# A two-layer diffusion backbone on one core: the first layer's feed-forward rebuilt as seven half-block products, with the gated blocks kept in DRAM

## The chip, the cores and the metric

The kernel runs on one core of one Trainium2 chip. The metric is the device time of one execution in microseconds; before the change the median of three runs is 3291.3 us (3287.67 to 3292.95).

## The reference, cut to what matters

Two layers act on 256 context tokens and 1024 latent tokens of width 1024, all in float32. Each layer has an attention, Fourier and recurrence part, and then a gated feed-forward (1024 to 2816 and back). The second layer updates the latent tokens only.

```python
def swiglu(h, wg, wu, wd):
    return (jax.nn.silu(h @ wg) * (h @ wu)) @ wd
for l in range(DEPTH):
    ctx_out = l < DEPTH - 1
    ...
    x = x + g_f * swiglu(rmsnorm(x) * (1 + sc_f) + sh_f, w_gate[l], w_up[l], w_down[l])
    if ctx_out:
        ctx = ctx + mc[5] * swiglu(rmsnorm(ctx) * (1 + mc[4]) + mc[3], w_gate[l], w_up[l], w_down[l])
return rmsnorm(x, final_norm)
```

## The kernel before, in words

Features lie on the 128 partitions and tokens on the free axis, so that the width is 8 tiles (KD) and the inner width 22 (NFF). Tokens come in three chunks (`CHUNKS`): chunk 0 is the context with 256 columns, chunks 1 and 2 are the latent tokens with 512 each. Every operand is split in two fp32r parts, hi and lo, by `split` (L124 to L126: a copy on ScalarE, then a subtraction on VectorE), and `mm3` (L128 to L134) makes three matmuls of each term: hi·hi, hi·lo and lo·hi. A weight block comes in by `slab` (L421): one DMA from the SyncE queue into a `raw` buffer, then the split into the `wh` and `wl` buffers. There are two `raw` buffers (RAWB) and four each of `wh` and `wl` (WB). A `raw` buffer is free again when the subtraction of its split has read it.

The kernel is written as a list of instructions in program order. A planner (the tile framework) puts them into one fixed order on each engine's queue, with the program order as priority and with its own estimates of durations; it inserts the waits, and it may put a DMA far ahead of its use when its buffer is free. The SyncE queue issues all DMAs, in its fixed order.

**Layer 0, feed-forward (`ffn`, L1057).** `out_proj` (L990) makes the residual stream `xT` in SBUF and the normalised operands `hh`, `hl`. Then 11 groups follow, each of 256 of the 2816 inner features. For each of its two 128-feature blocks and for each chunk a group makes `pg` and `pu` (8 terms of three matmuls each), the Silu, the gate product and its split. It then loads two rows of w_down and adds their two terms to each of the 8 output tiles of each chunk (`down`, accumulators `fd`); VectorE adds every such sum to `xT` (`add_residual`, L1049 to L1054). The last group is done in two parts, and the next layer's norm and first projections are put between them (`after`). Between the products, `next(bg)` advances `ada_sums` (L249): it streams 96 blocks of w_ada (256 KB each) through two `wa` buffers and sums them on VectorE (L279, L281), for the second layer's modulation vectors.

**Layer 1, feed-forward (`operands` L1143, `fast_product` L1230, `ffn_last` L1313).** Gate and up are products of a 1024 x 256 weight block with 1024 x 1024 latent activations. Both are cut into halves, and seven products of sums of half blocks stand for eight: B11, B21 and B22 are the activation halves themselves, and T1 to T4 are sums of them, made once in `operands`; sums of weight halves (`mix`) are made for each group. Each product is 4 terms of three 512-column matmuls. The gated results go to DRAM (`da`), and the residual stream does too (`df`). After all 11 groups, the down product is made in two passes, one per latent chunk: the 22 gated tiles come back (`ar`) and are split, and each of the 8 output tiles is accumulated over all 22 terms in one accumulator. The w_down blocks are loaded as slabs of 4 x 128 x 128 (256 KB; the last of each output tile is 128 KB), again in each pass.

```python
1323        for t in range(2):
...
1334            for ds in ((0, 1, 2, 3), (4, 5), (6, 7)) if t == 0 else ((0, 1), (2, 3), (4, 5), (6, 7)):
...
1336                for f0 in range(0, NFF, 4):
```

Of the kernel before, what the change touches and what calls it, by code (L numbers as in the profile page):

```python
# [92 lines left out]
LASTTAGS = ("mx", "sc", "mx", "mm")  # L93
# [7 lines left out]
class Kern:  # L101
# [304 lines left out]

    def norm_chunk(self, tag, l, vsc, vsh, ci, ss):
        self.modulate_chunk(l, vsc, vsh, ci, self.rstd(ss, CHUNKS[ci][1], D, f"{tag}r{ci}", "pa", PAB))
# [581 lines left out]
    def out_proj(self, l):  # L990
# [28 lines left out]
        def block(d, ci):  # L1019
            c0, n = CHUNKS[ci]  # L1020
            hi, lo = slabs[d]
            acc = self.ps("mm", "oacc")
            self.mm3(acc[:, :n], [(hi[k], lo[k], mh[k][:, c0:c0 + n], ml[k][:, c0:c0 + n]) for k in ORDER])
            self.add_residual(l, 2, d, ci, acc)
            self.squares(ss[ci], d, ci)
            if l + 1 == DEPTH:
                nc.sync.dma_start(out=self.df[d][:, c0 - CTX:c0 - CTX + n], in_=self.xT[d][:, c0:c0 + n])


        self.hh, self.hl = mh, ml  # L1030
        if l + 1 == DEPTH:
            for d in range(4):
                slab(d)
                for ci in chunks:
                    block(d, ci)
            self.operands(l, slab, block, ss)
            return
# [6 lines left out]
        for ci in chunks:  # L1044
# [10 lines left out]


    def ffn(self, l, bg, after):  # L1057
        nc = self.nc
        I = self.I
        chunks = (0, 1, 2)  # L1060

        groups = [(g, chunks, "") for g in range(NFF // 2 - 1)]
        groups += [(NFF // 2 - 1, chunks[:2], "last"), (NFF // 2 - 1, chunks[2:], "last")]

        def gate_up(g, i):
            f0 = (2 * g + i) * P
            return [self.slab(I[w][l, :, f0:f0 + P].rearrange("(k p) c -> p k c", p=P), f"{w}{l}_{f0}") for w in ("w_gate", "w_up")]

        first, norms = None, []
        for g, cis, last in groups:  # L1070
            A = {}
            for i in range(2):
                (gh, gl), (uh, ul) = first or gate_up(g, i)
                first = None
                if i and norms:
                    norms.pop()()
                for ci in cis:
                    c0, n = CHUNKS[ci]
                    cs = slice(c0, c0 + n)
                    pg, pu = self.ps("mm", "pg"), self.ps("sc", "pu")  # L1080
                    self.mm3(pg[:, :n], [(gh[k], gl[k], self.hh[k][:, cs], self.hl[k][:, cs]) for k in range(KD)])
                    next(bg, None)
                    self.mm3(pu[:, :n], [(uh[k], ul[k], self.hh[k][:, cs], self.hl[k][:, cs]) for k in range(KD)])
                    sg = self.t2("sg")
                    with self.tc.issue_after(self.last_exp):
                        self.last_silu = nc.scalar.activation(out=sg[:, :n], in_=pg[:, :n], func=AF.Silu).ins
                    nc.vector.tensor_tensor(out=sg[:, :n], in0=pu[:, :n], in1=sg[:, :n], op=ALU.mult)  # L1087
                    if i:
                        A[i, ci] = [self.t2(f"a{p}", F32R, tag="pa", bufs=PAB)[:, :n] for p in "hl"]
                    else:  # L1090
                        t = self.tp.tile([P, 2, 512], F32R, tag="qa", name="a", bufs=QAB)
                        A[i, ci] = [t[:, p, :n] for p in range(2)]
                    self.split(sg[:, :n], *A[i, ci])
                    next(bg, None)
            dn = []
            for i in range(2):
                f0 = (2 * g + i) * P
                dn.append(self.slab(I["w_down"][l, f0:f0 + P, :].rearrange("p (k c) -> p k c", c=P), f"wd{l}_{f0}"))
            tags = itertools.cycle(LASTTAGS)
            if last:  # L1100
                self.load = load = self.exp_ln_set(self.last_silu)

            def down(*blocks, o=0, n=None):
                accs = []
                for i in range(2):
                    for x, (d, ci) in enumerate(blocks):
                        nn = n or CHUNKS[ci][1]
                        if not i:
                            accs.append(self.ps(next(tags) if last else "mx" if ci else "pv", "fd"))
                        self.mm3(accs[x][:, :nn], [(dn[i][0][d], dn[i][1][d], *[y[:, o:o + nn] for y in A[i, ci]])], i == 0, i == 1)  # L1110
                        if i:
                            self.add_residual(l, 5, d, ci, accs[x], o, nn)

            if not last:
                for d in range(KD):
                    if d in (0, KD - 1):
                        down((d, 0), (d, 1), (d, 2))
                    else:
                        for ci in chunks:
                            down((d, ci))  # L1120
            else:
                ss = {}
                for ci in cis:
                    ss[ci] = self.square_acc(ci)
                    for d in range(KD):
                        down((d, ci))
                        self.squares(ss[ci], d, ci)
                if 2 in cis:
                    with self.tc.issue_after(load):
                        self.early_slabs(l + 1)  # L1130
                        self.early_chunk(l + 1, 1, slice(1))
                        norm = after(2, ss[2])
                        self.early_chunk(l + 1, 1, slice(1, 2))
                        norm()
                        self.early_chunk(l + 1, 2)
                else:
                    first = gate_up(g, 0)
                    with self.tc.issue_after(load):
                        norms = [after(ci, ss[ci]) for ci in cis]
                        norms.pop(0)()  # L1140


    def operands(self, l, slab, block, ss):  # L1143
# [21 lines left out]
        for d in range(4, KD):  # L1165
            slab(d)
            block(d, 1)
        slab(4)
        norm(1)
# [8 lines left out]
        puts = self.puts(0)  # L1178
        first = [self.fast_product(l, w, 0, *tb, put, True) for w, tb, put in zip(("w_gate", "w_up"), (("pa", PAB), ("t2", TB)), puts)]
# [33 lines left out]
    def puts(self, g):  # L1213
# [4 lines left out]
        def gate(i, t, x):  # L1218
            gates[i, t] = x
            with self.tc.issue_after(self.last_exp):  # L1220
                self.last_silu = nc.scalar.activation(out=x, in_=x, func=AF.Silu).ins

        def up(i, t, x):
            a = gates[i, t]
            nc.vector.tensor_tensor(out=a, in0=x, in1=a, op=ALU.mult)
            nc.sync.dma_start(out=self.da[2 * g + i][:, 512 * t:512 * t + 512], in_=a)
# [3 lines left out]
    def fast_product(self, l, w, g, tag, bufs, put, early=False):  # L1230


        nc, B = self.nc, self.B
        tags = itertools.cycle(("mm", "sc", "mx", "pv"))
# [31 lines left out]

        def result():
            return self.t2("m" + w, tag=tag, bufs=bufs)
# [5 lines left out]
        p = product(operand(A[0][0]), "11")  # L1274
        nc.scalar.copy(out=x, in_=p)
        p = product(operand(A[0][1]), "21")
        plus(z, p, x)
        if early:
# [8 lines left out]
        put(0, 0, z)  # L1287
# [11 lines left out]
        put(0, 1, v)  # L1299
# [6 lines left out]
        put(1, 1, y)  # L1306
# [4 lines left out]
        put(1, 0, x)  # L1311

    def ffn_last(self, l):  # L1313
        nc = self.nc
# [6 lines left out]
        load = self.exp_ln_set(self.last_silu)  # L1321
        tags = itertools.cycle(("mx", "pv"))
        for t in range(2):
            ts = slice(512 * t, 512 * t + 512)
            a = []
            for f in range(NFF):
                x = self.t2("ar", tag="pa", bufs=PAB)
                nc.sync.dma_start(out=x, in_=self.da[f][:, ts])
                y = self.five(f"a{t}_{f}", F32R, (P, 2, 512))
                a.append((y[:, 0], y[:, 1]))  # L1330
                self.split(x, *a[f])
            rows, X = [], []
            ss = self.t2("ssf", tag="acc", bufs=ACB)
            for ds in ((0, 1, 2, 3), (4, 5), (6, 7)) if t == 0 else ((0, 1), (2, 3), (4, 5), (6, 7)):
# [201 lines left out]
```

## Time and profile before

| what | value |
|---|---|
| median of three runs | 3291.3 us |
| the profiled execution's own time | 3293.05 us |
| its span in the profile | 3291.3 us |
| TensorE busy | 3193.4 us, 97% of the span |
| VectorE, ScalarE, GpSimd busy | 56%, 38%, 4% |
| mean granted TensorE clock | 0.988 |
| DMA | 303.89 MB, 92 GB/s on average |
| layer 0: output projection, feed-forward | from 780 us and from 911 us to about 1856 us |
| layer 1: output projection, feed-forward | from 2479 us and from 2573 us to the end |

The span is the time from the first instruction to the last. A matmul's recorded duration includes its way through the array, so the rate of a row of matmuls is read from the distance between their starts. A busy share near 100% says that the engine has work in its queue all the time; a granted clock below 1.00 says that matmuls then ran at a lower clock for a part of the stretch (1.00 is 2.4 GHz, 0.50 is 1.2 GHz).

### The profile page before, as it was taken

What the parts mean: (1) busy time and instruction counts of PE and PEld (TensorE: products, weight loads), DVE (VectorE), ACT (ScalarE), POOL (GpSimd) and SP (SyncE); (2) the same over time, 40 slices, a digit from 0 to 9 for tenths busy, and PEclk for the clock granted to TensorE, in tenths of its full rate; (3) what the DMA queues carried; (4) which work ended last, traced back from release to release, by engine and by line L of the source; (5) the groups of instructions that cost most, each with busy time, mean ns of one, the idle gap of its engine ahead of it and who ended that gap; (6) DMA issues with size and microseconds to landing.
All of it is one profiled execution on the core that took longest, in us unless ns stands there. A gap on an engine that the chain in (4) does not pass through costs nothing.

```text
span 3291.3 us, 43774 instructions
## 1 busy us (share of the span) xinstructions
PE 3193.4 (97%) x17074; PEld 2366.3 (72%) x17074; DVE 1844.6 (56%) x3230; ACT 1257.4 (38%) x2280; POOL 122.3 (4%) x96
## 2 busy tenths in 40 slices
PE   7999999998999999999999999999999899999998
PEld 4977544455878888888888787644557588887887
DVE  5298766653475353363334737677633876666343
ACT  5255555454331111111112635455453533334343
POOL 1000000000210000000000300000001100000000
PEclk9999999999999999999999999999999899999999
DMA  8346111024122141141112333210125132225453
GB/s 276 109 151 208 54 38 56 20 93 152 39 84 87 42 128 46 38 130 39 39 39 61 122 114 96 73 54 30 31 90 176 58 90 88 82 84 164 147 172 94
DMA packets 284408, 303.89 MB, mean 92 GB/s; under 512 B 16776, under 2 KB 207144, under 8 KB 284200
## 3 DMA queue, kind: packets, MB, share of 16 engines
q1 hardware_dynamic: 284200, 301.09, 29.1%
q8 instruction: 134, 2.20, 0.3%
q14 instruction: 74, 0.61, 0.1%
HBM read 237.18 MB, written 63.70 MB: 91 GB/s over the span
## 4 chain that ended last, share of the span: by engine, by line
PE 83%; DVE 7%; DMA 5%; ACT 3%; issue 2%; POOL 1%; SPq 0%; DVEq 0%; ACTq 0%; POOLq 0%
PE pv L643 6%; PE fd L132 5%; PE fd L133 5%; PE fd L134 5%; PE fp L133 4%; PE fp L132 4%; PE fp L134 4%; PE mx L600 3%; DMA wa<-in_w_ada_dram 3%; PE sm L648 3%; PE sc L634 3%; PE u L133 3%; PE u L132 3%; PE u L134 3%; PE pg L132 2%; PE pg L133 2%
## 5 line engine op out<-in xcount | busy, mean ns | idle before, releaser
L601 DVE TENSOR_REDUCE mp<-mx 128x1 f32<-128x512 f32 (+1 forms) x400 | 223.6, 589 | 131.1 <-PE mx L600 129.6
L637 ACT ACTIVATE p<-sc 128x512 f32<-128x512 f32 (+1 forms) x336 | 186.1, 586 | 186.9 <-PE sc L635 184.4
L132 PE MATMUL fd<-a,hwd 128*128 128x512 f32 (+1 forms) x616 | 234.2, 380 | 7.8 <-ACT hwd L125 6.8
L134 PE MATMUL fd<-a,lwd 128*128 128x512 f32 (+1 forms) x616 | 232.5, 377 | 1.4 <-DVE lwd L126 1.4
L133 PE MATMUL fd<-a,hwd 128*128 128x512 f32 (+1 forms) x616 | 233.1, 378 | 0.0
L643 PE MATMUL pv<-p,V 128*64 128x512 f32 (+1 forms) x672 | 230.6, 606 | 0.0
L1054 DVE SCALAR_TENSOR_TENSOR xT<-fd,mod,xT 128x512 f32<-128x512 f32 (+1 forms) x264 | 168.8, 659 | 83.5 <-PE fd L134 82.9
L279 DVE SCALAR_TENSOR_TENSOR as<-wa,sc,as 128x512 f32<-128x512 f32 x224 | 162.9, 753 | 62.5 <-DMA wa<-in_w_ada_dram 61.9
L132 PE MATMUL pg<-mh,hw_gate 128*128 128x512 f32 (+1 forms) x528 | 189.1, 358 | 4.4 <-DVE xT L1054 4.4
L126 DVE TENSOR_TENSOR lwd<-rwd,hwd 128x512 fp32r<-128x512 f32 (+1 forms) x144 | 96.7, 672 | 172.5 <-ACT hwd L125 169.7
L134 PE MATMUL pu<-mh,lw_up 128*128 128x512 f32 (+1 forms) x528 | 187.0, 354 | 0.9 <-DVE lw_up L126 0.8
L134 PE MATMUL pg<-mh,lw_gate 128*128 128x512 f32 (+1 forms) x528 | 187.9, 356 | 0.0
L133 PE MATMUL pg<-ml,hw_gate 128*128 128x512 f32 (+1 forms) x528 | 187.8, 356 | 0.0
L132 PE MATMUL pu<-mh,hw_up 128*128 128x512 f32 (+1 forms) x528 | 187.2, 355 | 0.0
L133 PE MATMUL pu<-ml,hw_up 128*128 128x512 f32 (+1 forms) x528 | 186.7, 354 | 0.0
L125 ACT CAST hwd<-rwd 128x512 fp32r<-128x512 f32 (+1 forms) x144 | 85.9, 597 | 207.5 <-PE fd L133 75.4
L1087 DVE TENSOR_TENSOR sg<-pu,sg 128x512 f32<-128x512 f32 (+1 forms) x66 | 39.6, 600 | 223.8 <-PE pu L134 223.8
L132 PEld LDWEIGHTS fd<-a,hwd 128*128 128x128 f32 x616 | 117.3, 190 | 32.5 <-ACT hwd L125 8.1
L125 ACT CAST hw_up<-rw_up 128x512 fp32r<-128x512 f32 x81 | 50.2, 621 | 225.7 <-PE fd L133 127.8
L132 PE MATMUL u<-a0hh,hwin 128*128 128x512 f32 (+1 forms) x360 | 132.3, 370 | 3.7 <-ACT a0hh L331 2.1
L133 PE MATMUL u<-a0hl,hwin 128*128 128x512 f32 (+1 forms) x360 | 129.1, 359 | 4.8 <-POOL a0hl L329 3.0
L134 PEld LDWEIGHTS fd<-a,lwd 128*128 128x128 f32 x616 | 116.8, 190 | 23.1 <-DVE lwd L126 2.1
(358 smaller groups left out, 7620.7 us busy)
## 6 DMA issues: line engine op xcount, KB each, us to landing
wa<-in_w_ada_dram SPq DMA_DIRECT2D x192, 256.0 KB
rw_gate<-in_w_gate_dram SPq DMA_DIRECT2D x46, 512.0 KB
rw_up<-in_w_up_dram SPq DMA_DIRECT2D x46, 512.0 KB
rwd<-in_w_down_dram SPq DMA_DIRECT2D x80, 256.0 KB
rwin<-in_w_in_dram SPq DMA_DIRECT2D x30, 512.0 KB
rwd<-in_w_down_dram SPq DMA_DIRECT2D x24, 512.0 KB
da<-mw_gate SPq DMA_DIRECT2D x44, 256.0 KB
ar<-da SPq DMA_DIRECT2D x44, 256.0 KB
```

Source lines behind the costliest of these rows:

```text
L125: self.nc.scalar.copy(out=hi, in_=src)
L132: self.nc.tensor.matmul(out, lh, rh, start=(first and i == 0), stop=False)
L133: self.nc.tensor.matmul(out, lh, rl, start=False, stop=False)
L134: self.nc.tensor.matmul(out, ll, rh, start=False, stop=(last and i == n - 1))
L279: nc.vector.scalar_tensor_tensor(out=acc, in0=w, scalar=sc, in1=acc, op0=ALU.mult, op1=ALU.add)
L600: nc.tensor.matmul(mx[:, :kn], Q1[a][:, t * P:(t + 1) * P], self.K1[g][:, k0:k0 + kn])
L601: nc.vector.tensor_reduce(out=mp[:, a * nt + t, i:i + 1], in_=mx[:, :kn], axis=AX.X, op=ALU.max)
L634: nc.tensor.matmul(sc[:, :n], self.K1[g][:, ks], Q1[a], start=True, stop=False)
L637: nc.scalar.activation(out=pf, in_=sc[:, :n], func=AF.Exp, scale=0.125)
L643: nc.tensor.matmul(pv[64 * a:64 * a + 64, :n], self.V[:, i, 64 * g:64 * g + 64], ps[i][a], start=(i == 0), stop=(i == nk - 1))
L648: nc.tensor.matmul(sm[r:r + 32, :n], self.c["first"], ps[i - 1 + o][a], start=(i == 1), stop=(i == nk - 1), tile_position=(0, r))
L1054: self.nc.vector.scalar_tensor_tensor(out=x, in0=acc[:, :n], scalar=self.mod[l][:, vec, d, s:s + 1], in1=x, op0=ALU.mult, op1=ALU.add)
```

## The change

The first layer's feed-forward takes the form of the second's. `out_proj` stores the residual to `df` in both layers and always ends in `operands`, which for layer 0 also makes the context's last four output blocks, its norm and its eight modulated operands. `fast_product` gets the context beside its seven products, as plain products over 256 columns (`context`), with one more weight split for each, since the block A[1][0] by itself is not an operand of the seven. `puts` stores gated blocks of all three chunks. The new `down_pass` holds what stood in `ffn_last`; layer 0 runs it three times (`down_next`: chunk 1, chunk 2, then the context), layer 1 twice (`down_last`). `ada_sums` is advanced once per slab in the first two passes and drained after the second. In the third pass, `todo` makes the next layer's normalised operands of chunks 2 and 1, one tile per slab.

```diff
@@ out_proj
-        for d in range(KD - 2):
+            nc.sync.dma_start(out=self.df[d][:, c0:c0 + n], in_=self.xT[d][:, c0:c0 + n])
+        for d in range(4):
             slab(d)
             for ci in chunks:
                 block(d, ci)
-        slab(KD - 2)
-        slab(KD - 1)
-        for ci in chunks:
-            block(KD - 2, ci)
-            block(KD - 1, ci)
-            self.norm_chunk(f"f{l}", l, 4, 3, ci, self.square_sum(ss[ci], ci))
+        self.hh, self.hl = mh, ml
+        self.operands(l, slab, block, ss)
@@ ffn: removed with its loop over groups, down() and after()
@@ operands
         for d in range(4, KD):
             slab(d)
+            if l == 0:
+                block(d, 0)
             block(d, 1)
...
+                if l == 0:
+                    self.modulate(self.xT[e][:, 0:CTX], rc[:, :CTX], e, 1, l, 4, 3, self.hh[e][:, 0:CTX], self.hl[e][:, 0:CTX])
@@ fast_product
+        def context(acc, parts, j, first):
+            if l == 0:
+                hi, lo = parts
+                self.mm3(acc, [(hi[:, k], lo[:, k], self.hh[4 * j + k][:, 0:CTX], self.hl[4 * j + k][:, 0:CTX]) for k in range(4)], first, not first)
...
+        if l == 0:
+            c = context_block()
+            context(c, a, 1, True)
+            context(c, operand(A[1][0]), 0, False)
+            put(1, 0, c)
@@ new
+    def down_pass(self, l, ci, groups, tags, take, step=lambda: None):
+        c0, n = CHUNKS[ci]
+        for f in range(NFF):
+            x = self.t2("ar", tag="pa", bufs=PAB)[:, :n]
+            nc.sync.dma_start(out=x, in_=self.da[f][:, c0:c0 + n])
...
+            self.split(x, *a[f])
+        for ds in groups:
+            accs = [self.ps(next(tags), "fd")[:, :n] for _ in ds]
+            for f0 in range(0, NFF, 4):
+                m = min(4, NFF - f0)
+                for d, acc in zip(ds, accs):
+                    hi, lo = self.slab(self.I["w_down"][l, P * f0:P * (f0 + m), d * P:(d + 1) * P].rearrange("(k p) c -> p k c", p=P), f"wd{l}_{ci}{d}_{f0}")
+                    self.mm3(acc, [(hi[k], lo[k], *a[f0 + k]) for k in range(m)], f0 == 0, f0 + m == NFF)
+                    step()
...
+    def down_next(self, l):
+        bg = self.ada_sums(l + 1, [(b, s) for b in range(4) for s in range(2)] + [(b, 0) for b in range(4, 12)], ("wa",) * WAB)
+        pairs = ((0, 1), (2, 3), (4, 5), (6, 7))
+        for ci in (1, 2, 0):
...
+            def take(d, x):
+                nc.sync.dma_start(out=self.dx[l + 1][d][:, cs], in_=x)
+                self.square_add(ss, d, x)
+            def step():
+                if ci:
+                    next(bg, None)
+                elif todo:
+                    todo.pop(0)()
...
+            self.down_pass(l, ci, ((0, 1, 2, 3), (4, 5), (6, 7)) if ci == 1 else pairs, tags, take, step)
+            if ci == 0:
+                with self.tc.issue_after(self.load):
+                    self.early_slabs(l + 1)
+                    self.early_chunk(l + 1, 1, slice(1))
...
+            if ci == 2:
+                for _ in bg:
+                    pass
+                self.new_h(f"a{l + 1}")
+                for d in range(KD):
+                    for c in (2, 1):
+                        todo.append(lambda d=d, c=c, x=X[d] if c == 2 else None: rows(d, c, x, R[c]))
+        with self.tc.issue_after(self.load):
+            self.early_chunk(l + 1, 1, slice(1, 2))
+            for d in range(KD):
+                rows(d, 0, X[d], R[0])
+            self.early_chunk(l + 1, 2)
```

## Rows read from the trace of the kernel before

**Rows 1.** The page: TensorE's busy time; the chain that ended last, by engine.
```profile
PE 3193.4 (97%) x17074; PEld 2366.3 (72%) x17074; DVE 1844.6 (56%) x3230; ACT 1257.4 (38%) x2280; POOL 122.3 (4%) x96
...
PE 83%; DVE 7%; DMA 5%; ACT 3%; issue 2%; POOL 1%; SPq 0%; DVEq 0%; ACTq 0%; POOLq 0%
```

**Rows 2.** Timeline, PE, layer 1: two starts, 12 matmuls of 512 columns apart.
```profile
3002.62 0.39 PE L132 MATMUL fp<-mh,hw_up 128*128 128x512 f32 x1
...
3005.34 0.39 PE L132 MATMUL fp<-mh,hw_up 128*128 128x512 f32 x1
```

**Rows 3.** Timeline, PE, layer 0: two starts, 12 matmuls of 256 columns apart.
```profile
1708.90 0.28 PE L132 MATMUL pg<-mh,hw_gate 128*128 128x256 f32 x1
...
1710.33 0.28 PE L132 MATMUL pg<-mh,hw_gate 128*128 128x256 f32 x1
```

**Rows 4.** Groups by form: first of each three matmul lines; count | busy us, mean ns | idle.
```profile
L132 PE MATMUL pg<-mh,hw_gate 128*128 128x512 f32 x352 | 137.9, 392 | 1.3 <-DVE xT L1054 1.3
...
L132 PE MATMUL pu<-mh,hw_up 128*128 128x512 f32 x352 | 137.1, 389 | 0.0
...
L132 PE MATMUL fp<-mh,hw_gate 128*128 128x512 f32 x176 | 69.7, 396 | 3.8 <-ACT hw_gate L125 3.0 <-ACT mh L1161 0.8
...
L132 PE MATMUL fp<-T,hw_gate 128*128 128x512 f32 x132 | 53.2, 403 | 4.6 <-ACT T L1161 3.4 <-ACT hw_gate L125 1.1
```

**Rows 5.** Windows, feed-forward starts, layer 1's groups: us, busy PE PEld DVE ACT POOL, PEclk, DMA, GB/s.
```profile
2584.00:2632.00 48.00, 33.26 (x86) 19.13 (x86) 39.03 (x59) 23.17 (x40) 8.30 (x4) 0.79 0.09 27
906.00:922.00 16.00, 11.61 (x58) 9.57 (x57) 14.82 (x19) 9.91 (x16) 5.87 (x4) 0.79 0.30 92
2715.00:2798.00 83.00, 83.00 (x368) 68.76 (x367) 56.24 (x90) 27.68 (x47) 0.00 (x0) 1.00 0.30 89
```

**Rows 6.** Windows, layer 1: end of gate and up, start of down, its first pass.
```profile
3014.00:3032.00 18.00, 18.00 (x81) 14.93 (x80) 14.11 (x23) 8.51 (x15) 0.00 (x0) 1.00 0.92 292
3032.00:3050.00 18.00, 11.16 (x37) 8.64 (x36) 9.64 (x15) 8.26 (x15) 0.00 (x0) 0.72 0.86 272
3062.00:3146.00 84.00, 83.86 (x377) 69.07 (x377) 38.01 (x60) 35.39 (x60) 0.00 (x0) 1.00 0.49 147
3146.00:3158.00 12.00, 12.00 (x57) 9.79 (x57) 9.19 (x15) 8.24 (x15) 0.00 (x0) 1.00 0.42 128
```

**Rows 7.** Windows, layer 0: the ten whole groups; two stretches at the feed-forward's end.
```profile
1836.00:1848.00 12.00, 7.81 (x31) 5.61 (x31) 10.64 (x13) 7.73 (x12) 4.58 (x3) 0.96 0.24 69
...
1866.00:1878.00 12.00, 9.97 (x40) 6.80 (x39) 9.42 (x11) 8.00 (x14) 7.65 (x5) 1.00 0.06 22
...
922.00:1800.00 878.00, 869.87 (x4535) 742.40 (x4535) 399.67 (x643) 154.52 (x272) 6.17 (x4) 1.00 0.22 65
```

**Rows 8.** The chain in order of time (start, us, what): one slab's load and copy.
```profile
3086.94 2.96 DMA rwd<-in_w_down_dram
...
3089.97 0.62 ACT hwd L125
```

**Rows 9.** Timeline, VectorE: that slab's subtraction.
```profile
3090.63 0.69 DVE L126 TENSOR_TENSOR lwd<-rwd,hwd 128x512 fp32r<-128x512 f32 x1 [0.88 <-ACT hwd L125]
```

**Rows 10.** Timeline, SyncE's queue, layer 1's first pass: slab issues in pairs (x2).
```profile
3042.96 1.13 SPq L425 DMA_DIRECT2D rwd<-in_w_down_dram  x2
...
3047.32 1.44 SPq L425 DMA_DIRECT2D rwd<-in_w_down_dram  x2
...
3052.22 1.39 SPq L425 DMA_DIRECT2D rwd<-in_w_down_dram  x2
```

**Rows 11.** Groups on the page: both `ada_sums`, VectorE's sums over w_ada.
```profile
L279 DVE SCALAR_TENSOR_TENSOR as<-wa,sc,as 128x512 f32<-128x512 f32 x224 | 162.9, 753 | 62.5 <-DMA wa<-in_w_ada_dram 61.9
```

**Rows 12.** Timeline, SyncE's queue, layer 0: seven w_ada loads in a row, two buffers.
```profile
1186.21 11.22 SPq L265 DMA_DIRECT2D wa<-in_w_ada_dram  x7
```

**Rows 13.** Windows, layer 1's operands: a stretch at the lower granted clock.
```profile
2602.00:2608.00 6.00, 5.36 (x13) 3.39 (x13) 5.43 (x8) 1.36 (x3) 0.67 (x1) 0.50 0.00 0
```

More of the change, by code (lines that the diff above doesn't have):

```diff
@@ L92 @@
 EARLYK = 4
-LASTTAGS = ("mx", "sc", "mx", "mm")
 ADASTEPS = (3, 7)
@@ L1054, in add_residual @@
         self.nc.vector.scalar_tensor_tensor(out=x, in0=acc[:, :n], scalar=self.mod[l][:, vec, d, s:s + 1], in1=x, op0=ALU.mult, op1=ALU.add)
[L1057 to L1140, printed above, removed]
@@ L1273, in fast_product @@
         x, z = result(), result()
-        p = product(operand(A[0][0]), "11")
+        a = operand(A[0][0])
+        p = product(a, "11")
         nc.scalar.copy(out=x, in_=p)
-        p = product(operand(A[0][1]), "21")
+        c = context_block()
+        context(c, a, 0, True)
+        a = operand(A[0][1])
+        p = product(a, "21")
         plus(z, p, x)
+        context(c, a, 1, False)
         if early:
@@ L1286, in fast_product @@
         nc.scalar.copy(out=y, in_=p)
-        put(0, 0, z)
+        put(0, 1, z)
+        if l == 0:
+            put(0, 0, c)
         S2 = mix(S1, A[0][0], ALU.subtract)
@@ L1298, in fast_product @@
         plus(v, p, v)
-        put(0, 1, v)
+        put(0, 2, v)
         S3 = mix(A[0][0], A[1][0], ALU.subtract)
@@ L1305, in fast_product @@
         plus(y, x, y)
-        put(1, 1, y)
+        put(1, 2, y)
         a = operand(A[1][1])
@@ L1320, in ffn_last @@
                 pass
-        load = self.exp_ln_set(self.last_silu)
+        self.load = self.exp_ln_set(self.last_silu)
+        (self.down_next if l + 1 < DEPTH else self.down_last)(l)
+    def down_pass(self, l, ci, groups, tags, take, step=lambda: None):
+        nc = self.nc
+        c0, n = CHUNKS[ci]
+        a = []
+        rooms = []
+        for f in range(NFF):
+            x = self.t2("ar", tag="pa", bufs=PAB)[:, :n]
+            nc.sync.dma_start(out=x, in_=self.da[f][:, c0:c0 + n])
+            for p in range(2):
+                if len(rooms) * (T // n) <= 2 * f + p:
+                    rooms.append(self.five(f"a{l}{ci}_{f}", F32R, (P, T // n, n)))
+            a.append([rooms[(2 * f + p) // (T // n)][:, (2 * f + p) % (T // n)] for p in range(2)])
+            self.split(x, *a[f])
[7 more added lines that the diff above has]
+                    step()
+            for d, acc in zip(ds, accs):
+                if d % 2 == 0:
+                    pair = self.tp.tile([P, 2, 512], F32, tag="qa", name="xo", bufs=QAB)
+                x = pair[:, d % 2, :n]
+                nc.sync.dma_start(out=x, in_=self.df[d][:, c0:c0 + n])
+                nc.vector.scalar_tensor_tensor(out=x, in0=acc, scalar=self.mod[l][:, 5, d, (ci == 0):(ci == 0) + 1], in1=x, op0=ALU.mult, op1=ALU.add)
+                take(d, x)
@@ L1322, in ffn_last, with down_last @@
+    def down_last(self, l):
+        nc = self.nc
         tags = itertools.cycle(("mx", "pv"))
         for t in range(2):
[L1324 to L1332, printed above, removed]
@@ L1358, in ffn_last, with take @@
-            self.final(t, rows, r)
-    def rows_out(self, tags, x0, x1):
+            ss = self.t2("ssf", tag="acc", bufs=ACB)
+            rows, X, R = [], [], []
+            def take(d, x):
+                self.square_add(ss, d, x)
+                nc.scalar.activation(out=x, in_=x, func=AF.Copy, scale=self.gain("final_norm", d))
+                X.append(x)
+                if d == 7:
+                    with self.tc.issue_after(self.load):
+                        R.append(self.final_rstd(ss))
+                if d % 4 == 3:
+                    rows.append(self.rows_out(("mx", "pv") if t and d == 7 else ("mm", "sc"), X[-4:]))
@@ L1363, in rows_out @@
+            self.down_pass(l, 1 + t, ((0, 1, 2, 3), (4, 5), (6, 7)) if t == 0 else ((0, 1), (2, 3), (4, 5), (6, 7)), tags, take)
+            self.final(t, rows, R[0])
+    def rows_out(self, tags, X):
         pts = [self.ps(tags[t % 2], "xop") for t in range(4)]
@@ L1429, in run @@
                 self.mixers(l)
-            if l + 1 == DEPTH:
-                self.ffn_last(l)
-                break
-            bg = self.ada_sums(1, [(b, s) for b in range(4) for s in range(2)] + [(b, 0) for b in range(4, 12)], ("wa",) * WAB)
-            def after(ci, ss):
-                c0, n = CHUNKS[ci]
-                if ci == 0:
-                    for _ in bg:
-                        pass
-                r = self.rstd(self.square_sum(ss, ci), n, D, f"a1r{ci}", "pa", PAB)
-                def rest():
-                    self.modulate_chunk(1, 1, 0, ci, r)
-                    if ci:
-                        for d in range(KD):
-                            nc.sync.dma_start(out=self.dx[1][d][:, c0:c0 + n], in_=self.xT[d][:, c0:c0 + n])
-                return rest
-            self.ffn(l, bg, after)
+            self.ffn(l)
     def mixers(self, l):
```

98 lines of the change are left out of this document (49 added, 49 removed).

## The prediction

> **What bounds the kernel now.** I read the page first: TensorE is busy for 97% of the span and makes 83% of the chain that ended last [rows 1]. So a change pays by what it takes from TensorE's queue, and costs what it makes TensorE wait. Next came the groups by form, for the number of matmuls, and the timeline, for their rate. Twelve matmuls of 512 columns start 2.72 us apart, 0.2267 us each [rows 2]; twelve of 256 columns 1.43 us apart, 0.12 us each [rows 3]. Last came windows, on the places where layer 1 already does what layer 0 is to do. There a stretch's length less its matmuls at 0.2267 us is what was lost.
>
> I sum against the profiled execution (3293.05 us), which lies 1.75 us above the median of the runs. A measurement of this kernel can tell about 0.2%, 6.6 us, from no change.
>
> **Products saved: -60 us.** Layer 0 has three lines of 352 matmuls for `pg` and as many for `pu`, 2112 of 512 columns; layer 1 has three lines of 176 + 132 each for gate and for up, 1848 [rows 4]. So 264 x 0.2267 us = 59.8 us go. The context's matmuls and all of the down product's keep their number and widths. The extra weight split (one copy and one subtraction for each weight block of a group) is hidden: in layer 1's groups VectorE was busy for 56 of 83 us and ScalarE for 28, with TensorE never idle [rows 5], and layer 0 takes 24.8 us for a block (84 x 0.2267 + 48 x 0.12) where layer 1 takes 19.0.
>
> **Start of the feed-forward: +20 us.** In layer 1, making T1 to T4 leaves TensorE waiting for VectorE: 48 us hold 86 matmuls, worth 19.5 us, so 28 us are lost, a part of it to a granted clock of 0.79 [rows 5]. In layer 0 now, norm and first products lose less: 4.4 us idle in 16 us, and the clock at 0.79 there, some 7 to 8 us [rows 5]. The difference is 20 us. Layer 0's context products (2 x 24 x 0.12 = 5.8 us before T1 is needed) can fill some of the wait, and its eight context tiles add to VectorE, which is busy for 39 of the 48 us. Bounds +12 and +30.
>
> **Start of the down product: +10 us.** The last gated blocks go to DRAM and come back, behind 22 `ar` loads in a saturated queue (DMA share 0.92, 292 GB/s): 18 us hold 37 matmuls, worth 8.4 us, so 9.6 us are lost in layer 1 [rows 6]. Layer 0 gets the same. It has a little more context work at the end to cover it, and `ada_sums` loads beside it. Bounds +5 and +18.
>
> **Waits that go from the old loop: -9 us.** The ten groups were idle for 878 - 869.87 = 8.1 us, and a little more went with the clock after it [rows 7]. Bounds -8 and -13.
>
> **The third pass: +38 us.** This is the term that decides. The context is 256 columns wide, so a slab of w_down feeds only 12 x 0.12 = 1.44 us of matmuls, against 2.72 us in the other passes, and all 48 slabs of w_down come in again. Two `raw` buffers hold the loads. One buffer's round is the load (2.96 us from issue), ScalarE's copy (0.62) and VectorE's subtraction (0.69), 4.3 us in all [rows 8, 9]. With two buffers that is a slab every 2.15 us. The queue shows it at work: issued in pairs at 3042.96, 3047.32 and 3052.22, two slabs took 4.36 and 4.90 us, 2.2 to 2.45 us each [rows 10]. I take 2.2, since the third pass has less other traffic. Forty full slabs lose 0.76 us each, 30 us; the eight half slabs have no row of their own, and between no loss and a full slab's round (2.2 - 0.72 us, 12 us in all) I take 1 us each. The sum is 38 us on 63 us of matmuls. Bounds: 30, and 60 if each slab takes 2.7 us. Nothing covers it: TensorE's queue holds only that pass there, and the `todo` steps add VectorE and ScalarE work (16 tiles, and eight loads of chunk 1's residual) behind which a slab's split must queue.
>
> By the Trainium skill, DMA: Bandwidth & Descriptors, Anatomy of one DMA, a load costs about 2.0 us and its bytes at 436 GB/s (fitted there for the other issuing path), which is an estimate of 2.6 us for a slab; the third pass would then lose about 9 us less. The trace's 2.96 us is higher, and it goes into the sum.
>
> **Passes one and two: +12 us.** Layer 1's first pass, with the same 2.72 us a slab, ran 84 us with 0.14 us idle, and so did the seam between its passes [rows 6]. So slabs alone cost nothing. But the 96 w_ada loads move from the groups, where the DMA share was 0.22 [rows 7], into these 240 us. Their traffic there is two w_down (23.1 MB), w_ada (25.2), 44 `ar` (11.5) and 32 stores and loads of the residual (8.4): 68 MB, 284 GB/s. The saturated stretch gave 292 GB/s at 0.92 [rows 6], so the share is about 0.9. VectorE gets the w_ada sums too, 0.753 us each, half of the 224 for this layer, 84 us [rows 11]. In the queue seven of these loads took 11.2 us, 1.6 us each [rows 12], in runs that slab loads and their subtractions must share. Where a slab's round goes from 4.3 to 5.6 us (2.8 us a slab), TensorE starts to wait. I take 5% of 240 us. Bounds 0 and +40.
>
> **Seams and end: +4 us.** After the second pass `ada_sums` is drained and `new_h` takes 16 of the 25 large buffers, so the third pass's operands get buffers only as the second's last group frees them: some 4 us (0 to 12), with layer 1's seamless change of pass as the low end [rows 6]. The end, where the next norm is waited for, lost 4.2 and 2.0 us in layer 0 [rows 7]; the new one has the same chain in another order, 0 (-8 to +8).
>
> **Sum.** -60 + 20 + 10 - 9 + 38 + 12 + 4 = +15 us: 3293 + 15 = 3308 us, 3306 us by the median.
>
> **Rivals.**
> *The slab stream keeps up.* If slabs come early enough for the third pass (loads put far ahead, or a shorter round) and the w_ada loads find gaps, 38 and 12 us fall away: 3306 - 50 = 3256 us. For it speaks layer 1's first pass, without a wait at 147 GB/s [rows 6]; against it, that it needs a slab only every 2.72 us, while the third pass needs one in 1.44 us and two buffers gave 2.2 [rows 10]. The point of decision is 1.44 us a slab; half way there, with low ends elsewhere, the change is still a gain of some 20 us. Chance 0.30 for a gain over 0.2%.
>
> *The third pass runs at the lower clock.* In it TensorE would work for 1.44 us and wait for 0.8 us, 48 times. Layer 1's operands had waits of this kind: the granted clock fell to 0.50 (1.2 GHz), with 13 matmuls in 5.36 us of work, 0.41 us each [rows 13]. At 0.24 us for 256 columns a full slab takes 2.9 us and the pass loses 40 x (2.9 - 1.44) + 8 x 0.7 = 64 us, 26 more: 3332 us. Against it, the kernel's mean clock is 0.988, and the waits are short. Chance 0.15, part of it together with 30 to 40 us lost to a saturated DMA in passes one and two. [...]
>
> *The saving isn't there.* If sums of halves cost TensorE more than 1/8, or VectorE held up the groups, up to 60 us would be missing. Layer 1's 1848 matmuls at 0.2267 us show the contrary [rows 4, 2]; chance 0.02.
>
> **How the numbers follow.** The forecast, with 3285 to 3330 us of its own, has 0.50 (of which 0.43 lie over 0.2% slower), the first rival and low ends 0.33 (0.30 faster), the clock 0.15, the missing saving 0.02. No change within 0.2% gets 0.10, from the forecast's low end and the first rival's high one. That gives 0.30 faster, 0.10 same, 0.60 slower. The range from 3258 to 3345 us leaves out one in ten on either side.
>
> **What would show it.** Right: 1848 + 1848 matmuls of `fp` with 512 columns; third-pass windows with TensorE busy for some 60% and slabs of 2.2 us; SyncE waiting there for VectorE's `lwd`; a DMA share near 0.9 in passes one and two; a stretch like layer 1's 48 us at the feed-forward's start. Wrong: a third pass of 65 to 75 us, or no idle time after the products, and the time is near 3256 us. A clock of 0.5 to 0.7 in the third pass would be the second rival.

## The result and the profile after

The changed kernel takes 3315.85 us (median of four runs, 3308.07 to 3316.72) where the one before takes 3290.82 us (four runs). The ratio is 1.0072, with a 95% interval from 1.0054 to 1.0089: slower by 25 us. The forecast was 3306 us, slower, with a range from 3258 to 3345 us.

The profiled execution spans 3313.5 us, 22.2 us more than before. First its page: TensorE's busy time and the chain by engine, which answer to [rows 1], and the costliest group of the down product with the idle time before it.

```profile
PE 3170.5 (96%) x16810; PEld 2335.8 (70%) x16810; DVE 1977.4 (60%) x3463; ACT 1394.4 (42%) x2526; POOL 104.5 (3%) x77
...
PE 79%; DMA 8%; DVE 7%; ACT 3%; issue 2%; POOL 0%; SPq 0%; ACTq 0%; DVEq 0%; POOLq 0%
...
L131 PE MATMUL fd<-a,hwd 128*128 128x512 f32 (+1 forms) x880 | 338.0, 384 | 34.3 <-ACT hwd L124 34.3
```

TensorE's busy time is 23 us less and the kernel takes 22 us more: it waits. (Of the 60 us of matmuls that went only 23 show in the busy time, probably because matmuls at the lower clock are recorded as longer, and because before a wait the way of the last one through the array counts as well.) In the chain DMA has gone from 5% to 8%. The down product's first matmul of a term waits 34.3 us for ScalarE's copy of a weight slab. Before, the two groups on that line, both layers' `a` and layer 0's `ah`, waited 7.8 and 6.7 us, and the 6.7 not for a slab but for the gated operand:

```profile
L132 PE MATMUL fd<-a,hwd 128*128 128x512 f32 (+1 forms) x616 | 234.2, 380 | 7.8 <-ACT hwd L125 6.8
...
L132 PE MATMUL fd<-ah,hwd 128*128 128x512 f32 (+1 forms) x264 | 94.5, 359 | 6.7 <-ACT ah L125 6.7
```

The groups by form of the changed kernel, answering to [rows 4], show that the saving came:

```profile
L131 PE MATMUL fp<-mh,hw_gate 128*128 128x512 f32 x352 | 140.3, 399 | 7.7 <-ACT hw_gate L124 4.0 <-ACT mh L1058 3.7
...
L132 PE MATMUL fp<-T,hw_gate 128*128 128x512 f32 x264 | 106.3, 403 | 6.7 <-DVE T L1059 6.7
```

Both layers together have 352 + 264 matmuls on each of three lines for gate and as many for up, which is 2 x 1848. The 264 matmuls are gone from layer 0.

Windows of the changed kernel's layer 0 show where the time went. Columns: the stretch, its us, busy us of TensorE (number), weight loads, VectorE, ScalarE, GpSimd, granted clock, DMA share, GB/s. The lines are the start of the feed-forward, the groups, the start of the down product, passes one and two in two parts, and the third pass in three.

```profile
901.00:965.00 64.00, 48.40 (x201) 34.06 (x199) 50.50 (x79) 34.52 (x62) 17.91 (x7) 0.89 0.15 46
1000.00:1476.00 476.00, 476.00 (x2538) 412.49 (x2537) 272.05 (x435) 145.76 (x251) 0.00 (x0) 1.00 0.24 75
1476.00:1500.00 24.00, 13.62 (x55) 10.44 (x54) 19.41 (x31) 14.13 (x23) 0.00 (x0) 0.84 0.94 309
1500.00:1634.00 134.00, 126.27 (x529) 99.26 (x528) 94.56 (x157) 46.90 (x81) 0.00 (x0) 0.95 0.76 235
1634.00:1760.00 126.00, 120.13 (x517) 95.09 (x515) 73.82 (x128) 36.88 (x73) 0.00 (x0) 0.99 0.74 223
1760.00:1776.00 16.00, 11.52 (x62) 8.50 (x63) 11.01 (x21) 8.73 (x15) 0.00 (x0) 0.79 0.60 181
1776.00:1800.00 24.00, 15.45 (x92) 13.88 (x91) 24.00 (x29) 14.92 (x26) 10.92 (x7) 0.85 0.54 161
1800.00:1880.00 80.00, 63.35 (x391) 56.11 (x390) 29.48 (x50) 24.17 (x45) 1.38 (x2) 0.87 0.42 122
```

The groups run without any idle time at full clock, as layer 1's do. The rest is in the down product: 14 us idle in the 260 us of passes one and two with the DMA share at 0.75, and 30 us idle in the third pass with a granted clock of 0.79 to 0.87 on average, a mix of its two levels.

I count lost time as the distance between the starts of successive matmuls beyond the rates of [rows 2, 3], summed over a stretch; unlike idle time it holds what a lower clock costs. By that count the first 100 us of the feed-forward lose 27 us, the first 64 us of the down product 13, the rest of passes one and two 24, and the time from the context's first matmul (1759.1 us) to layer 1's first (1880.5 us) 55 us.

Three views say what the slabs wait for. SyncE's queue in the third pass shows eight slab loads in a row without another DMA between them:

```profile
1826.95 15.79 SPq L421 DMA_DIRECT2D rwd<-in_w_down_dram  x8
```

The eighth starts 15.4 us after the first, so a slab goes out every 2.2 us. (From 1794 to 1873 us it is 36 loads, 2.3 us each, six of them half slabs.) The chain in order of time of 1826 to 1846 us, its shares by line and one round of a buffer (start, us, what), has hardly any TensorE in it; the next load of a slab goes out only after the subtraction:

```profile
by line: DMA rwd<-in_w_down_dram 65.2%; DVE lwd L125 17.6%; ACT hwd L124 12.5%; PE fd L133 3.1%; issue 2.2%; PE fd L132 1.9%; PE fd L131 1.8%; ACTq L124 0.8%
...
1829.20 2.86 DMA rwd<-in_w_down_dram
...
1832.15 0.63 ACT hwd L124
...
1832.81 0.70 DVE lwd L125
```

The third view is the waits of SyncE's queue (what waited, for whom: us in total, times, longest), first from 1772 to 1880 us, in the third pass, where a load waits until its buffer's last load has landed and the subtraction has read it:

```profile
SPq L421 <- DVE lwd L125: 38.6, 34, 2.4
SPq L421 <- DMA rwd<-in_w_down_dram: 20.6, 17, 2.2
```

Then in passes one and two:

```profile
SPq L421 <- DVE lwd L125: 59.0, 75, 1.8
SPq L264 <- DVE as L278: 37.5, 58, 1.7
```

The issue of a slab load (L421) waits for VectorE's subtraction, which frees the `raw` buffer, and the issue of a w_ada load (L264) for VectorE's sum. A load that stands behind either waits too. Slab loads also take longer there than the 2.96 us of [rows 8]; two of those in the chain:

```profile
1548.22 6.26 DMA rwd<-in_w_down_dram
...
1618.62 5.33 DMA rwd<-in_w_down_dram
```

### The profile page after: what moved, and what is told of

It reads as the page before. It is cut to its first block, busy times and chain, and to the rows that moved or that the text cites. A ratio compares the mean times of both kernels' runs of the same rounds, so it can differ in the third digit from the quotient of the medians.

```text
span 3313.5 us, 44692 instructions
## 1 busy us (share of the span) xinstructions
PE 3170.5 (96%) x16810; PEld 2335.8 (70%) x16810; DVE 1977.4 (60%) x3463; ACT 1394.4 (42%) x2526; POOL 104.5 (3%) x77
## 4 chain that ended last, share of the span: by engine, by line
PE 79%; DMA 8%; DVE 7%; ACT 3%; issue 2%; POOL 0%; SPq 0%; ACTq 0%; DVEq 0%; POOLq 0%
PE fp L131 8%; PE fp L132 8%; PE fp L133 8%; PE pv L639 6%; PE fd L133 3%; PE fd L131 3%; PE fd L132 3%; PE mx L596 3%; DMA rwd<-in_w_down_dram 3%; PE sm L644 3%; PE sc L630 3%; PE u L131 3%; PE u L132 3%; PE u L133 3%; PE sc L631 2%; DMA wa<-in_w_ada_dram 2%
## 5 line engine op out<-in xcount | busy, mean ns | idle before, releaser
L131 PE MATMUL fd<-a,hwd 128*128 128x512 f32 (+1 forms) x880 | 338.0, 384 | 34.3 <-ACT hwd L124 34.3
L132 PE MATMUL fd<-a,hwd 128*128 128x512 f32 (+1 forms) x880 | 333.9, 379 | 0.1
L131 PEld LDWEIGHTS fd<-a,hwd 128*128 128x128 f32 x880 | 174.0, 198 | 70.8 <-ACT hwd L124 40.6
L133 PEld LDWEIGHTS fd<-a,lwd 128*128 128x128 f32 x880 | 173.8, 198 | 55.5 <-DVE lwd L125 27.7
L132 PEld LDWEIGHTS fd<-a,hwd 128*128 128x128 f32 x880 | 173.9, 198 | 30.2 <-issue 1.9
L131 PE MATMUL fp<-mh,hw_gate 128*128 128x512 f32 x352 | 140.3, 399 | 7.7 <-ACT hw_gate L124 4.0
L133 PE MATMUL fp<-mh,lw_gate 128*128 128x512 f32 x352 | 139.5, 396 | 4.4 <-DVE lw_gate L125 4.4
L132 PE MATMUL fp<-ml,hw_gate 128*128 128x512 f32 x352 | 140.0, 398 | 1.6 <-DVE ml L1059 1.5
L131 PE MATMUL fp<-mh,hw_up 128*128 128x512 f32 x352 | 138.4, 393 | 0.2 <-ACT hw_up L124 0.2
L132 PE MATMUL fp<-ml,hw_up 128*128 128x512 f32 x352 | 137.5, 391 | 0.0
L133 PE MATMUL fp<-mh,lw_up 128*128 128x512 f32 x352 | 137.2, 390 | 0.1
L131 PE MATMUL oacc<-mh,hwo 128*128 128x512 f32 (+1 forms) x320 | 122.2, 384 | 9.8 <-ACT mh L124 8.4
L133 PE MATMUL u<-a0hh,lwin 128*128 128x512 f32 (+1 forms) x360 | 127.8, 356 | 0.0
```

The source lines that it names most:

```text
L131: self.nc.tensor.matmul(out, lh, rh, start=(first and i == 0), stop=False)
L132: self.nc.tensor.matmul(out, lh, rl, start=False, stop=False)
L133: self.nc.tensor.matmul(out, ll, rh, start=False, stop=(last and i == n - 1))
```

## The experiments

Times are medians, and ratios are to the kernel before on the same chip, with 95% intervals. The runs were made on several chips, so two kernels are compared by their ratios.

**Wide slabs in the third pass.** One DMA brings the slabs of two output tiles into one `raw` buffer:

```diff
+    def slab2(self, src, name):
+        nk = src.shape[1]
+        raw = self.wp.tile([P, nk, 2 * P], F32, tag="raw", name="r" + name, bufs=RAWB)
+        self.nc.sync.dma_start(out=raw, in_=src)
+        out = []
+        for i in range(2):
+            hi, lo = self.piece(f"{name}_{i}", nk)
+            self.split(raw[:, :, P * i:P * i + P], hi, lo)
...
+                    if not (ci == 0):
                         hi, lo = self.slab(self.I["w_down"][l, P * f0:P * (f0 + m), d * P:(d + 1) * P].rearrange("(k p) c -> p k c", p=P), f"wd{l}_{ci}{d}_{f0}")
+                    elif d % 2 == 0:
+                        both = self.slab2(self.I["w_down"][l, P * f0:P * (f0 + m), d * P:(d + 2) * P].rearrange("(k p) c -> p k c", p=P), f"wd{l}_{ci}{d}_{f0}")
+                        hi, lo = both[0]
+                    else:
+                        hi, lo = both[1]
```

> The third pass (context, 48 slabs) took 108 us after the change, where its matmuls alone are 63 us. This kernel loads the slabs of two output tiles in one DMA in that pass alone, so that two raw buffers hold four slabs. Theory (the round of two raw buffers sets the pace, 2.25 us a slab): the pass shrinks to 75 to 82 us and the time falls by about 28 us, to 3288 us (below before). Rival 1 (the lower TensorE clock sets the pace, and the waits come with it): the pass stays above 95 us, time above 3303 us. Rival 2 (VectorE, which is full for the first 24 us of the pass with the next norm's tiles, sets the pace): only the later part shrinks, the pass is 90 us or more and the time about 3300 us.

Measured: 3283.24 us, ratio 0.9986 (0.9976 to 0.9995), 28 us less than the change and a little below before. From the context's first matmul to layer 1's first it is 89 us where it was 121, and 23 us are lost where it was 55. (The expectation's 108 us are those from 1772 to 1880 us; the pass's first matmul stands at 1759.1 us.) The windows of its third pass:

```profile
1760.00:1776.00 16.00, 13.97 (x95) 11.95 (x94) 13.33 (x24) 11.02 (x20) 2.27 (x1) 0.89 0.71 219
1776.00:1800.00 24.00, 17.93 (x115) 16.27 (x114) 22.98 (x30) 15.65 (x29) 9.43 (x7) 0.86 0.59 182
1800.00:1846.00 46.00, 42.58 (x335) 40.45 (x333) 22.54 (x40) 17.70 (x36) 1.66 (x2) 1.00 0.58 179
```

Its slab loads in SyncE's queue, in the same columns as the changed kernel's:

```profile
1811.45 13.09 SPq L441 DMA_DIRECT2D rwd<-in_w_down_dram  x6
```

The sixth starts 12.7 us after the first. Any six loads in a row hold one of half slabs, here the fourth, with 256 KB where the others have 512; so nine slabs' bytes went out in that time, 1.41 us a slab. That is about the 1.44 us of a slab's matmuls: the loads keep up and follow TensorE. The size of the fourth, and the chain's shares from 1811 to 1824 us:

```profile
rwd<-in_w_down_dram SPq DMA_DIRECT2D x1, 256.0 KB
...
by line: PE fd L133 35.0%; PE fd L132 30.4%; PE fd L131 29.4%; DVE lwd L125 5.4%; issue 0.4%
```

In the last 46 us TensorE is busy for 42.6 us at full clock. So the round of two `raw` buffers set the pace, and the lower clock came with the waits and went with them. A wide slab changes two things, half as many loads and twice the bytes in two buffers; more buffers of one slab were not tried. Of the 23 us that are left, 16 lie before 1800 us, where VectorE is still full.

**No w_ada loads.** The sums over w_ada are left out of passes one and two:

```diff
-        bg = self.ada_sums(l + 1, [(b, s) for b in range(4) for s in range(2)] + [(b, 0) for b in range(4, 12)], ("wa",) * WAB)
+        bg = iter(())
+        self.mod[l + 1] = self.cst.tile([P, 6, KD, 2], F32, name=f"mod{l + 1}")
+        nc.vector.memset(self.mod[l + 1], 0.5)
```

> This kernel leaves the second layer's modulation sums out: the 96 w_ada loads and VectorE's sums in passes one and two are gone, and the modulation vectors are set to 0.5. The first two passes took 296 us after the change, where their matmuls are 239 us, of which 10 us are lost at the start. Theory (the w_ada loads and sums share the DMA engines, SyncE's queue and VectorE with the slabs): passes one and two lose 5 us or less after their start, and the time falls by about 30 us, to 3286 us. Rival (the slabs, the gated blocks coming back and the residual's loads and stores alone are too much): at least half of the loss stays, the time is above 3300 us. The start of the down product keeps some 8 to 10 us of loss under both.

Measured: 3276.86 us, ratio 0.9971 (0.9959 to 0.9982), 33 us less than the change. Windows of its passes, start and rest:

```profile
1477.00:1500.00 23.00, 13.54 (x55) 10.78 (x55) 15.43 (x24) 13.09 (x22) 0.00 (x0) 0.79 0.87 279
1500.00:1733.00 233.00, 230.96 (x1010) 190.32 (x1010) 99.57 (x165) 83.18 (x154) 0.00 (x0) 0.99 0.52 159
```

The rest of the two passes takes 233 us where it took 260, with 2 us idle, and loses 4 us by distances where it lost 24. The DMA share falls from 0.75 to 0.52. The rival is out: slabs, gated blocks and the residual's traffic cost hardly anything by themselves. Waits in SyncE's queue are no loss by themselves either; without the sums its slab loads wait longer there than the 59.0 us with them, and TensorE hardly waits after the start:

```profile
SPq L421 <- DVE lwd L125: 127.6, 84, 2.8
```

The first 64 us of the down product lose 11 us where it was 13; most of that loss isn't the sums'. The run takes away the sums' loads, their work on VectorE and their places in SyncE's queue together, so it doesn't say which of these cost the time.

**The next norm's tiles spread.** One in every third slab, not one with each of the first 16:

```diff
-                elif todo:
-                    todo.pop(0)()
+                else:
+                    count[0] += 1
+                    if todo and count[0] % 3 == 0:
+                        todo.pop(0)()
```

> The next norm's 16 tiles are made one every third slab of the third pass, and not one with each of its first 16 slabs. Theory (two raw buffers' round sets the pace all through the pass, and VectorE's full first 24 us add a little): 4 to 8 us less, about 3310 us. Rival 2 of the run with wide slabs (VectorE's work there sets the pace): 12 us less or more, 3303 us or below. If the tiles come too late for the first projection after the pass, it is slower.

Measured: 3307.64 us, ratio 1.0062 (1.0047 to 1.0077). The interval overlaps that of the change, so the time alone shows nothing. The trace has 117.5 us from the context's first matmul to layer 1's first, 4 less; but the kernel without the sums has 115 us there with the tiles as in the change, so the 4 us can't be put down to the tiles. This run's windows of the pass, whose first 24 us now have VectorE at 16.85 us:

```profile
1757.00:1781.00 24.00, 17.40 (x112) 13.72 (x112) 16.85 (x28) 12.19 (x21) 1.75 (x2) 0.86 0.61 179
1781.00:1874.00 93.00, 69.58 (x431) 60.25 (x431) 46.51 (x70) 35.45 (x65) 11.22 (x7) 0.91 0.46 133
```

VectorE is relieved and the pass stays long: it wasn't what set the pace.

**The sums in the groups.** `ada_sums` goes on during gate and up of layer 0, two sums at a time in the one free large buffer:

```diff
+            if size == 2:
+                room = self.five(f"as{l}", F32, (P, 2, 512))
+                accs = [room[:, 0], room[:, 1]]
...
     def ffn(self, l):
+        bg = self.bgf = self.ada_sums(l + 1, [(b, s) for b in range(4) for s in range(2)] + [(b, 0) for b in range(4, 12)], ("wa",) * WAB, 2) if l + 1 < DEPTH else iter(())
...
             for _ in self.fast_product(l, "w_gate", g, "pa", PAB, gate):
-                pass
+                next(bg, None)
+            next(bg, None)
...
```

> The second layer's modulation sums go on during the eleven groups of gate and up of layer 0, two sums at a time in the one free large buffer, and not in the first two down passes. Theory (the groups leave the DMA engines at 0.24 and VectorE at 57%, the passes have no room): passes one and two lose 5 us or less after their start, the groups lose 3 to 8 us, the time falls by 20 to 28 us, to 3288 to 3296 us. Rival (the sums cost the same wherever they stand, since VectorE's queue makes weight splits wait behind them): the groups lose 20 us or more, and the time stays above 3305 us.

Measured: 3292.51 us, ratio 1.0013 (1.0003 to 1.0022), 19 us less than the change (1.0072 less 1.0013, of 3290 us). Windows of its groups, and of passes one and two after their start:

```profile
1002.00:1494.00 492.00, 492.00 (x2607) 416.20 (x2606) 339.28 (x554) 151.21 (x262) 0.00 (x0) 1.00 0.39 118
...
1518.00:1746.00 228.00, 227.54 (x1003) 187.80 (x1003) 97.52 (x163) 81.04 (x152) 0.00 (x0) 1.00 0.53 160
```

The passes take 228 us with 0.5 us idle. From the feed-forward's first matmul to the down product's, the groups take 17 us more, of which 7 us are lost by distances; the rest is the sums' own matmuls, which only moved. So the sums have room in the groups and little in the passes.

**Both, and wide slabs everywhere.** The first of these runs joins wide slabs in the third pass with the sums in the groups. The second also has wide slabs in all five passes (`if not (True)` in place of `if not (ci == 0)`) and the spread tiles.

> Wide slabs in the third pass and the modulation sums in the groups, together. Theory (two separate losses, one in the third pass by the round of the raw buffers, one in the first two by the w_ada loads): the savings add, 28 + 19 us off the changed kernel, ratio to before 0.993, about 3264 us. Rival (they are one shortage of DMA or VectorE that the two share): clearly less than the sum, ratio 0.996 or more.

Measured: 3261.48 us, ratio 0.9930 (0.9915 to 0.9945). The change's 1.0072 less 0.0086 and 0.0059 is 0.9927: the savings add, so they are two separate losses.

> As the run with both, with wide slabs in all five down passes and the next norm's tiles one every third slab. Theory: passes one and two hardly waited any more with the sums gone, so wide slabs there bring 0 to 3 us; spreading the tiles brings some 3 us as it did alone. Ratio to before 0.991 to 0.993, 3258 to 3264 us. Rival (512 KB loads land later and hurt at the start of each down product, where TensorE waits for the first slab): 3 to 8 us slower than the run with both.

Measured: 3252.76 us, ratio 0.9901 (0.9882 to 0.9919), and in another set of runs 3251.09 us, 0.9894 (0.9879 to 0.9908). In microseconds that is more of a gain than expected; by ratio the first interval reaches the expected 0.991, and the second ends just below it. Windows of the start of the down product, of passes one and two, and of the third:

```profile
1492.00:1516.00 24.00, 20.81 (x93) 16.77 (x92) 16.81 (x29) 14.77 (x25) 0.00 (x0) 1.00 0.91 298
1516.00:1736.00 220.00, 220.00 (x971) 181.68 (x970) 95.40 (x160) 80.53 (x150) 0.00 (x0) 1.00 0.51 164
1736.00:1817.00 81.00, 72.83 (x528) 68.56 (x527) 54.48 (x84) 42.93 (x80) 12.37 (x8) 0.94 0.60 187
```

The same start with narrow slabs in passes one and two (the run with both), and once more with wide ones (the other set of runs):

```profile
1492.00:1516.00 24.00, 15.52 (x63) 12.31 (x61) 16.69 (x28) 14.67 (x24) 0.00 (x0) 0.86 0.90 294
```

```profile
1496.00:1520.00 24.00, 18.86 (x78) 15.23 (x78) 16.35 (x28) 14.35 (x25) 0.00 (x0) 0.90 0.85 277
```

Where the change fits 55 matmuls into the first 24 us of the down product and the run with both 63, this kernel fits 93 and 78, at a higher clock. So the rival had the sign wrong: with two buffers holding four slabs, TensorE has more to do while the last gated blocks come back. The third pass is 81 us and 79 us where the run with both has 85. By the ratios this kernel is 33 to 35 us faster than the one before, and 56 to 59 us faster than the change.

**The start of the feed-forward.** Three runs ask why TensorE waits where T1 to T4 are made. All go out from the kernel with wide slabs everywhere.

> As the run with wide slabs everywhere, with two of the four subtractions that split T1 moved from VectorE to GpSimd, in both layers. Theory (VectorE's chain makes TensorE wait where T1 to T4 are made, 27 us in each layer): 2 to 6 us less. Rival (each step waits for the one before it, and GpSimd takes 1.7 us or more where VectorE takes 0.7): no change, or up to 4 us slower.

```diff
-            put("T1", T1[k], self.hh[k][:, c2], self.hl[k][:, c2])
+            put("T1", T1[k], self.hh[k][:, c2], self.hl[k][:, c2], nc.gpsimd if k % 2 else nc.vector)
```

Measured: 3250.93 us, ratio 0.9899 (0.9883 to 0.9914), the same; the first 100 us lose 30.0 us where the kernel it starts from loses 28.8.

Then the chain in order of time of the changed kernel (start, us, what) pointed elsewhere: GpSimd's subtraction for T3 stands in it, and ScalarE's copy of its result ahead of the copy for T1 (`mh`).

```profile
924.72 4.57 POOL xT L1105
929.32 0.62 ACT T L1058
929.94 0.53 ACT mh L1058
```

> The kernel with wide slabs everywhere, the modulation sums in the groups and the tiles spread, again, beside the next run. Ratio to before 0.990, with 28 us lost in the first 100 us of layer 0's feed-forward, most of it before T4.

Measured: 3251.09 us, as told above, with 30.7 us lost in the first 100 us of layer 0's feed-forward.

> As the run beside it, with the subtraction that makes T3 moved from GpSimd to VectorE in both layers. In the changed kernel's trace the first of them took 4.57 us on GpSimd, and ScalarE's copy of its result stood in its queue ahead of T1's copies. Theory (that GpSimd step, too early in ScalarE's queue, is what holds T1 and T2 up, and not VectorE's amount of work): the 27 to 28 us lost at the start of each layer's feed-forward fall to 18 to 24, the time by 4 to 15 us. Rival (VectorE's amount of work sets the time, and gets four subtractions more): no change, or 3 us slower.

```diff
-            nc.gpsimd.tensor_tensor(out=v[k], in0=v[4 + k], in1=v[k], op=ALU.subtract)
+            nc.vector.tensor_tensor(out=v[k], in0=v[4 + k], in1=v[k], op=ALU.subtract)
```

Measured: 3248.32 us, ratio 0.9879 (0.9862 to 0.9895), against 0.9894 for the kernel beside it; the intervals overlap. The first 100 us of layer 0's feed-forward lose 29.3 us (30.7 beside it). That theory falls: the step is in the chain, but without it other work holds TensorE as long.

> As the kernel with wide slabs everywhere, but the eight VectorE subtractions that make T2 and T4 from their halves are left out in both layers (the halves themselves are used, with every split and product kept). Theory (VectorE's amount of work holds TensorE at the start of each layer's feed-forward, 0.68 us an operation): the first 70 us lose 22 to 26 us where they lost 28 to 30. Rival (the loss is in the lower clock and in single long waits): 27 us or more.

```diff
-            nc.vector.tensor_tensor(out=T1[k], in0=v[4 + k], in1=T1[k], op=ALU.subtract)
-            put("T2", T1[k], q[:, 0], q[:, 1])
+            put("T2", v[4 + k], q[:, 0], q[:, 1])
...
-            nc.vector.tensor_tensor(out=u[4 + k], in0=u[4 + k], in1=T1[k], op=ALU.subtract)
```

Measured: one run, 3243.27 us, beside one of the kernel before with 3283.61. In the first 70 us, layer 1 loses 24.1 us (29.3 and 31.2 in the two runs of the kernel it starts from) and layer 0 27.7 (28.5 and 29.8). The same window of both kernels, first with the subtractions left out, then with them (the first one's feed-forward begins 3 us earlier):

```profile
901.00:965.00 64.00, 51.51 (x207) 38.32 (x208) 49.15 (x76) 32.25 (x57) 10.10 (x5) 0.84 0.18 52
```

```profile
901.00:965.00 64.00, 47.25 (x200) 34.64 (x198) 52.80 (x82) 34.13 (x61) 17.91 (x7) 0.92 0.18 53
```

Layer 1 goes with VectorE's amount of work, layer 0 doesn't. With VectorE at 49 to 53 of 64 us, neither the amount of work nor one step of the chain explains it alone. What holds TensorE there stays open.

## Why the prediction was right, point by point

The sign and its reason were right: the saved products came, and what layer 0 takes over with layer 1's form costs more. Against the forecast's +15 us on the profiled execution stand +22 (and +25 between the medians). A part of that nearness is luck: terms that came out dearer make +28 us against the forecast, and terms that came out cheaper or were not in it make -22. By lost time the terms are:

- **Products saved, -60 us:** as forecast. 264 matmuls are gone, and the groups run without a wait.
- **Start of the feed-forward, +20 us:** 27 us lost where the kernel before lost 9.5 (its matmuls from 880 to 922 us), +18. The size held, taken over from layer 1's window; its cause, VectorE, is only half shown.
- **Start of the down product, +10 us:** 13 us.
- **Waits that go, -9 us:** the old loop lost 14 us between 922 and 1800 us by distances, so -14, just outside the bounds. Idle time alone undercounts, since the clock after a wait isn't in it.
- **Third pass and seam, +38 and +4 us:** 55 us. The mechanism and its pace were right: 2.2 us a slab, and wide slabs took 32 us away, against 38 for the round alone. The rest of the 55 us lies mostly in the pass's first 40 us, where the seam and the norm's tiles are, behind which the splits queue. That work was named in the term and given no price, and how the loss divides there isn't shown. The sign of TensorE being busy for some 60% did not come: it is 75% from 1760 to 1880 us.
- **Passes one and two, +12 us:** this is the term that was mis-sized. It came to 24 us by distances, and to some 27 by the passes' length with and without the sums. I took 5% of 240 us for a DMA share of 0.9; 10% would have been right, at a measured share of 0.75, so the share alone was no measure of the price. The loads, the sums and the slabs share the DMA engines, SyncE's queue and VectorE, and which of these cost the time isn't shown.
- **End, 0 us:** from 1800 us on, the old end and the first 34 us of layer 1 lost 13 us; the new layer 1's first 34 us, from 1880 us on, lost 2. That is -11, outside the bounds of -8 and +8. The output projection also lost 4 us less, which was not in the sum.

With these, -60 + 18 + 13 - 14 + 24 + 55 - 11 - 4 = +21 us, where the spans differ by 22.

The first rival, a slab stream that keeps up, is what the wide slabs make: the loads came at TensorE's pace, 1.41 us a slab beside its point of decision of 1.44 us, and with the sums out of the way the ratio came to 0.993, where its 3256 us would be 0.989. The second, the lower clock, was there (0.79 to 0.87 on average, not 0.50), but as a companion of the waits: it was gone in the last 46 us of the pass with wide slabs. The Trainium skill (TensorE: Matmul & The Clock Gate, HAM oscillation) tells of a loop whose wait for each tile's load is longer than its work, and whose clock falls at every wait. The trace agrees in direction, though the waits here are shorter than the work (some 0.8 us to 1.44 us): the clock fell for a part of the pass, and not throughout.

## What to carry to other kernels

When a product is cut into passes over the same weights, work out for each pass what one weight block feeds: a pass half as wide needs its blocks twice as fast, and two buffers give one block in half a round (load, copy and subtraction), whatever the DMA engines could carry. Put two blocks into a buffer before adding passes, and leave background loads in the stage where the queue has room: they are not free in every stage to which a rewrite moves them.

## What the runs showed of the hardware that was not expected

In the chains of the third pass a load of two slabs (512 KB) took 3.54 us from issue to landing where one of one slab (256 KB) took 2.86 us: twice the bytes for a quarter more time. (Single loads took longer, up to 4.33 us for two slabs and 4.53 us for one.) The load of one slab stands with the changed kernel's chain above, this is the one with wide slabs:

```profile
1805.41 3.54 DMA rwd<-in_w_down_dram
```

GpSimd's 128x512 subtraction took 4.57 us next to a busy VectorE, 6 to 7 times VectorE's 0.69 us (the three after it 3.3 us each), and doing without it changed the time by less than the runs can tell.
